# A hybrid backbone block on one core: the first channel tile's shift and scale columns are loaded apart, and the opening order of the tensor engine is rewritten

## The chip, the cores and the metric

The kernel runs on one core of one Trainium2 chip. The time is the device time of one execution in microseconds (us); the figure for the kernel before is the median of three runs. The engines are named as in the profile: PE is TensorE (matrix products), PEld its weight loads, DVE is VectorE, ACT is ScalarE, POOL is GpSimd, SP is SyncE, which here issues nearly all loads. SPq stands for its queue of load instructions.

## What is computed

One layer of a diffusion backbone over 512 latent tokens and 256 context tokens, model width 2048, all in 32-bit floats. Only the opening matters here:

```python
c_act = silu(c); cc_act = silu(c_ctx)
mod   = c_act  @ w_mod + b_mod          # 6 x 2048: sh1, sc1, gt1, sh2, sc2, gt2
mod_c = cc_act @ w_mod + b_mod
h  = rmsnorm(x,   g_norm1) * (1 + sc1)  + sh1
hc = rmsnorm(ctx, g_norm1) * (1 + csc1) + csh1
lat_in = h  @ w_in                      # q, k, v of 8 heads, gates
ctx_in = hc @ w_in
...
```

Behind it come two kinds of scans over the heads, an output projection, and a feed-forward part with a 3x3 convolution. They make up most of the time and are not touched.

## The kernel before

**Layout.** Channels lie on the 128 partitions: the 2048 channels are 16 channel tiles, numbered k, or 8 pairs, numbered kp. `xl[k]` is a tile of the 512 latent tokens (128 channels by 512 tokens), `xc[k]` one of the 256 context tokens. A product in full precision is made of three faster ones: each operand is split into a high part (a cast on ACT, `S.copy`, line 89) and a low part (a subtraction on DVE, line 90), and `mm3` adds high by high, high by low and low by high. In the profile `hTh` and `hTl` are the parts of the modulated latent tokens, `hch` and `hcl` those of the context, `hi_h` and `lo_h` those of a pair's weights of one head (`load_split`, line 160, 512 KB each).

**Order.** `pinned[0] = True` around `project_first` (lines 523 to 525) makes every product keep its program order on PE. So on PE what is written first runs first, and whatever stands behind a waiting product waits too. The other engines' order is set by the framework's scheduler, which prefers what stands under `tc.high_priority()`; `tc.issue_after(ins)` puts the instructions of a block behind `ins` on the engine of `ins`. Loads are issued by SP in program order; each needs a free buffer of its pool (`wraw` 4, `mraw` 7).

**The opening, in order.** (1) Three small loads (`cv`, a part of the constants, `cols`; lines 466 to 468) and then the 16 latent token tiles go out on SP (line 473). (2) `stream_rstd` (line 485): ACT squares each tile, DVE adds the squares up (`sq_l`, line 86), one product with a matrix of ones sums over channels (`ss_l`), and ACT and DVE turn the sum into `rl`, the reciprocal root for each token (`rstd` in the profile). (3) The shift and scale of a channel tile are needed as columns, one number for each partition. They come as rows first: `mod_rows` (line 221) multiplies the two condition vectors with 256 columns of `w_mod`, that is of one pair of channel tiles, in 32 instructions on PE (`ps_m`), and ACT copies the result to `rows_m`; `mod_cols` (line 234) transposes it with a small product for each tile, and DVE writes `scol` (scale, region 1) or `shcol` (shift, region 0). One `mod_load` (line 213) is four loads of 512 KB, for one region and one pair. (4) `modulate` (line 502) multiplies a tile by `rl`, applies scale and shift (line 510), and splits it. (5) Products: head 1 is accumulated pair by pair in banks that are evicted after each pair (`early_group`, `early_pair`; `psB`, two banks), head 0 in six banks that stay (`project_chunk`; `psA`, six banks). Groups 0 and 1 are q and k, groups 2 and 3 the latent v, groups 4 and 5 the context. `a` in the profile is any bank of a head.

In `project_first` (line 365) both regions of pair 0 are done first, then 8 products that nothing reads (line 379, they multiply ones with `rl`), then head 1's pair 0 groups 0 to 3, then head 0's, with the rows and columns of pair 1 and the context's sum (`ss_c`) set between them:

```python
        early_pair(w1, sums)
        for g in range(2, 4):
            early_group(0, g, w1, sums)
        project_chunk(0, *w0, banks[0], 0)
        rows = mod_rows(1, 1, raws[1])
        project_chunk(0, *w0, banks[1], 1)
        mod_cols(1, 1, *rows)
        ...
        rows = mod_rows(0, 1, raws[0])
        early_group(0, 4, w1, sums)
        mod_cols(0, 1, *rows)
        early_group(0, 5, w1, sums)
```

Then come the groups 4 and 5 of head 0 with the scale of pair 2, and a loop over pairs 1 to 7 with all six groups of head 1 and then of head 0 in each round. The shift and scale of the pairs ahead are set between the groups, some groups before they are needed.

Of the kernel before, what the change touches and what calls it, by code (L numbers as in the profile page):

```python
# [11 lines left out]
F32 = mybir.dt.float32  # L12
# [57 lines left out]
def block_kernel(ctx: ExitStack, tc: tile.TileContext, a: dict, out: bass.AP):  # L70
# [150 lines left out]
    def mod_rows(region, n, raws):  # L221

        bank = psb(f"ps_m{region}_{n}")
        ps = bank[:, 0:256]
# [4 lines left out]
        rows = tmp.tile([P, 256], F32, name=f"rows_m{region}_{n}", tag="rows")  # L229
# [4 lines left out]
    def mod_cols(region, n, bank, rows):  # L234
# [4 lines left out]
        with tc.high_priority():  # L239
            for b in range(2):  # L240
                k = 2 * n + b
                if region == 1:
                    V.tensor_scalar(out=scol[:, k, :], in0=pc[:, b, :], scalar1=bp1[:, k : k + 1],
                                    scalar2=gn1[:, k : k + 1], op0=ALU.add, op1=ALU.mult)
                else:
                    V.tensor_scalar(out=shcol[:, k, :], in0=pc[:, b, :], scalar1=bmod[:, k : k + 1],
                                    scalar2=None, op0=ALU.add)
# [61 lines left out]
    def project_chunk(kp, wh, wl, o, g, first=0, last=KT - 1):  # L309

        ks = list(enumerate((2 * kp, 2 * kp + 1)))
# [41 lines left out]
    def early_pair(w, sums):  # L353

        (wh, wl), ps = w, [psb(f"a1_0_{g}", BANKS[g]) for g in range(2)]
        for n, (ws, xs) in enumerate(((wh, hx[0]), (wl, hx[0]), (wh, hx[1]))):
            for k in range(2):
                for g in range(2):
                    mm(ps[g], ws[:, k, P * g : P * g + P], xs[k], start=(n == 0 and k == 0), stop=(n == 2 and k == 1))
        for g in range(2):  # L360
            sums[g] = actp.tile(list(BANKS[g]), F32, name=f"e0_{g}", tag=f"ah{KT - 4 + g}")
            with tc.high_priority():
                S.activation(sums[g], ps[g], AF.Copy, scale=SCALE if g == 0 else 1.0)

    def project_first():

        banks = [acc(f"a0_{g}", BANKS[g]) for g in range(6)]
        sums = [None] * 4 + [accp.tile([P, DK + DV], F32, name=f"e0_{4 + j}", tag=f"sum{j}") for j in range(CJ)]
        stream_rstd(xl, rl, "l", T)
        for r in (1, 0):  # L370
            mod_cols(r, 0, *mod_rows(r, 0, mod_load(r, 0)))
        w1, w0 = (load_split(a["w_heads"][h, 0], f"h{h}_0") for h in (1, 0))
        for j in range(KT // 2):
            nc.sync.dma_start(xcp[j], a["ctxT"][j])
        raws = {r: mod_load(r, 1) for r in (1, 0)}
        with tc.high_priority():
            ins = modulate(0, "x")

        for _ in range(8):
            mm(banks[5][:, 0:P], ones, rl[:, 0:P], start=True, stop=True)  # L380
        early_pair(w1, sums)
        for g in range(2, 4):
            early_group(0, g, w1, sums)
        project_chunk(0, *w0, banks[0], 0)
        rows = mod_rows(1, 1, raws[1])
        project_chunk(0, *w0, banks[1], 1)
        mod_cols(1, 1, *rows)
        with tc.high_priority(), tc.issue_after(ins):
            stream_rstd([x.rearrange("p a b -> p (a b)") for x in xcp], rc, "c", TC)
            ins = modulate(0, "c")  # L390
        for g in range(2, 4):
            project_chunk(0, *w0, banks[g], g)
        rows = mod_rows(0, 1, raws[0])
        early_group(0, 4, w1, sums)
        mod_cols(0, 1, *rows)
        early_group(0, 5, w1, sums)
# [3 lines left out]
        for r in (1, 0):  # L400
            raws[r] = mod_load(r, 2)
        nc.sync.dma_start(cst[:, 0:C_SA], a["consts"][:, 0:C_SA])
        project_chunk(0, *w0, banks[4], 4)
        rows = mod_rows(1, 2, raws[1])
        project_chunk(0, *w0, banks[5], 5)
        mod_cols(1, 2, *rows)
        for kp in range(1, KP):
            for g in range(6):
# [862 lines left out]
```

## Time and profile before

| | |
|---|---|
| three runs | 2586.46 to 2589.58 us, median 2588.95 |
| the profiled execution | 2584.39 us, its span from first to last instruction 2582.7 |
| mean granted clock of PE | 0.998 |
| DVE, ACT busy | 54%, 31% of the span |
| DMA over the span | 321.35 MB, mean 124 GB/s |
| chain of work that ended last | PE 91%, DVE 4%, DMA 2%, ACT 1%, issue 1% |

A row of the timeline has the start in us from the beginning of the span, the duration, the engine, the line, the operation, what it writes and reads, shapes and count; brackets hold the idle time of the engine before it and what released it. Matrix products are pipelined: the recorded duration of one is longer than the distance to the next. The line of every product is that of the helper `mm` (line 95), so products are told apart by their tiles. A product of 32-bit floats that aren't split takes two instructions.

### The profile page before, as it was taken

To read this page: it belongs to the slowest core of one execution; us is meant where nothing else is said; L and a number is where in the kernel's file an instruction comes from. 1 tells how busy PE (TensorE), PEld (TensorE's weight loads), DVE (VectorE), ACT (ScalarE), POOL (GpSimd) and SP (SyncE) were. 2 spreads that over 40 slices of the span, in tenths; PEclk is the share of its full clock that TensorE was granted. 3 is DMA by queue.
4 is the path that set the end of the run, shared out by engine and by line. 5 is a ranking of instruction groups with operands and counts; after the bars stand their busy time and mean duration, and the time that the engine had idled before them with its cause. 6 is when DMAs were issued, how large, how long until landed. Compare 5 with 4: busy or idle time off the path is not lost.

```text
span 2582.7 us, 31755 instructions
## 1 busy us (share of the span) xinstructions
PE 2533.8 (98%) x12944; PEld 2123.4 (82%) x12944; DVE 1400.4 (54%) x2055; ACT 811.3 (31%) x1209; POOL 78.5 (3%) x85
## 2 busy tenths in 40 slices
PE   6999999999999999999999999999999999999998
PEld 4887899888887888887788888888888888888887
DVE  6557765554445676459765336533653365336534
ACT  4224543322223242234533123312331233123332
POOL 0000000000000000002500000000000000000001
PEclk9999999999999999999999999999999999999999
DMA  9740011132335676324722222222232222222323
GB/s 383 273 156 34 33 42 50 42 122 98 114 115 186 245 266 239 131 85 147 272 97 97 98 98 98 95 96 95 98 98 98 98 98 93 95 97 87 105 94 106
DMA packets 96345, 321.35 MB, mean 124 GB/s; under 512 B 10884, under 2 KB 15304, under 8 KB 96200
## 3 DMA queue, kind: packets, MB, share of 16 engines
q1 hardware_dynamic: 95112, 318.29, 35.7%
q8 instruction: 101, 1.65, 0.3%
q10 hardware_dynamic: 1088, 1.05, 0.1%
q14 instruction: 44, 0.36, 0.0%
HBM read 315.10 MB, written 4.19 MB: 124 GB/s over the span
## 4 chain that ended last, share of the span: by engine, by line
PE 91%; DVE 4%; DMA 2%; ACT 1%; issue 1%; POOL 0%; SPq 0%; DVEq 0%; ACTq 0%; POOLq 0%
PE ug L95 17%; PE a L95 17%; PE dn L95 17%; PE uv L95 16%; PE ga L95 7%; PE wo L95 7%; PE po L95 3%; DMA raw_m<-in_w_mod 2%; PE ps_m L95 1%; PE sl L95 1%; PE dl L95 1%; DVE cv L1102 1%; DVE sum_m L268 0%; PE cst L95 0%; DVE sq_l L86 0%
## 5 line engine op out<-in xcount | busy, mean ns | idle before, releaser
L95 PE MATMUL uv<-h2h,lo_uv 128*128 128x512 f32 x688 | 268.1, 390 | 3.4 <-DVE lo_uv L90 3.4
L95 PE MATMUL ug<-h2h,lo_ug 128*128 128x512 f32 x688 | 266.7, 390 | 2.0 <-DVE lo_ug L90 2.0
L95 PE MATMUL uv<-h2h,hi_uv 128*128 128x512 f32 x688 | 267.8, 389 | 0.0
L95 PE MATMUL uv<-h2l,hi_uv 128*128 128x512 f32 x688 | 267.7, 389 | 0.0
L95 PE MATMUL ug<-h2h,hi_ug 128*128 128x512 f32 x688 | 267.5, 391 | 0.1
L95 PE MATMUL ug<-h2l,hi_ug 128*128 128x512 f32 x688 | 266.5, 389 | 0.0
L95 PE MATMUL dn<-gl,hi_d 128*128 128x512 f32 x644 | 250.6, 389 | 0.0
L95 PE MATMUL dn<-gh,hi_d 128*128 128x512 f32 x644 | 250.6, 389 | 0.0
L95 PE MATMUL dn<-gh,lo_d 128*128 128x512 f32 x644 | 250.6, 389 | 0.0
L1102 DVE SCALAR_TENSOR_TENSOR cv<-pad,cwt,cv 128x512 f32<-128x512 f32 x344 | 243.4, 762 | 9.0 <-ACT cv L1100 7.7
L90 DVE TENSOR_TENSOR lo_ug<-raw_ug,hi_ug 128x1024 fp32r<-128x1024 f32 (+1 forms) x88 | 106.9, 1214 | 254.9 <-ACT hi_ug L89 254.9
L90 DVE TENSOR_TENSOR lo_uv<-raw_uv,hi_uv 128x1024 fp32r<-128x1024 f32 (+1 forms) x88 | 109.8, 1247 | 176.3 <-ACT hi_uv L89 175.9
L268 DVE SCALAR_TENSOR_TENSOR sum_m<-raw_m,csil,sum_m 128x512 f32<-128x512 f32 x208 | 161.3, 775 | 55.6 <-DMA raw_m<-in_w_mod 51.4
L90 DVE TENSOR_TENSOR lo_d<-raw_d,hi_d 128x1024 fp32r<-128x1024 f32 x82 | 98.7, 1204 | 166.1 <-ACT hi_d L89 165.2
L89 ACT CAST hi_ug<-raw_ug 128x1024 fp32r<-128x1024 f32 (+1 forms) x88 | 90.8, 1032 | 276.3 <-PE ug L95 202.2
L89 ACT CAST hi_d<-raw_d 128x1024 fp32r<-128x1024 f32 x82 | 85.1, 1037 | 279.1 <-PE dn L95 224.4
L89 ACT CAST hi_uv<-raw_uv 128x1024 fp32r<-128x1024 f32 (+1 forms) x88 | 90.8, 1032 | 244.4 <-PE uv L95 182.0
L95 PEld LDWEIGHTS uv<-h2h,lo_uv 128*128 128x128 f32 x688 | 129.1, 188 | 31.6 <-DVE lo_uv L90 5.0
L95 PEld LDWEIGHTS ug<-h2h,lo_ug 128*128 128x128 f32 x688 | 129.1, 188 | 29.7 <-DVE lo_ug L90 2.8
L95 PEld LDWEIGHTS ug<-h2h,hi_ug 128*128 128x128 f32 x688 | 129.1, 188 | 27.9 <-issue 0.8
L95 PEld LDWEIGHTS uv<-h2l,hi_uv 128*128 128x128 f32 x688 | 129.1, 188 | 26.8
L95 PEld LDWEIGHTS uv<-h2h,hi_uv 128*128 128x128 f32 x688 | 129.1, 188 | 26.7
(312 smaller groups left out, 5018.6 us busy)
## 6 DMA issues: line engine op xcount, KB each, us to landing
raw_m<-in_w_mod SPq DMA_DIRECT2D x192, 512.0 KB, 4.6
raw_ug<-in_w_up SPq DMA_DIRECT2D x80, 512.0 KB, 3.2
raw_uv<-in_w_up SPq DMA_DIRECT2D x80, 512.0 KB, 3.3
raw_d<-in_w_down SPq DMA_DIRECT2D x79, 512.0 KB, 3.3
raw_h<-in_w_heads SPq DMA_DIRECT2D x64, 512.0 KB, 3.4
raw_ga<-in_w_gates SPq DMA_DIRECT2D x32, 512.0 KB, 3.5
raw_wo<-in_w_out SPq DMA_DIRECT2D x32, 512.0 KB, 3.2
xl<-in_xT SPq DMA_DIRECT2D x16, 256.0 KB, 5.4
```

The costliest lines, as they stand in the source:

```text
L89: S.copy(hi, x)
L90: return V.tensor_tensor(out=lo, in0=x, in1=hi.bitcast(F32), op=ALU.subtract).ins
L95: ins = PE.matmul(*args, **kw)
L268: V.scalar_tensor_tensor(out=dv, in0=x, scalar=ck, in1=dv, op0=ALU.mult, op1=ALU.add)
L1102: V.scalar_tensor_tensor(out=t3, in0=src, scalar=w, in1=t3, op0=ALU.mult, op1=ALU.add)
```

## The change

It does these things in `project_first` and its helpers, and in the three small loads:

- The three small loads are issued from ACT's queue (`nc.scalar.dma_start`) instead of SP's.
- Twelve products that nothing reads, on the first 256 tokens of latent tiles 2 to 13, are put ahead of `stream_rstd`.
- The rows of pair 0 are made tile by tile. A second arrangement of the same weights, `w_mod0`, holds them as two loads of 512 KB for each region and tile; `mod_half` makes rows of 128 columns and transposes them. Tile 0's loads stand ahead of the head weights, tile 1's behind them.
- `unread` products (three in each `mod_half` of tile 0, eight behind it) multiply ones with `rl`, as the eight of before did.
- With tile 0 alone come the products of head 0, groups 0 to 3, and of head 1, groups 0 and 1; then tile 1's rows, columns, modulation (`modulate_x`) and the same products again. Head 1's groups 0 and 1 take two `psA` banks for this.
- The context's sum and modulation are ordered behind tile 1's. Pair 1's scale is made and transposed between group 3 of head 1 and group 4 of head 0; its shift around the last group of head 1. Pair 2's scale moves into the loop's first round, and the load of pair 2's shift with it.

```diff
-    def mod_rows(region, n, raws):
+    def mod_load_half(region, k):
+
+        raws = []
+        for i in range(2):
+            pl = wraw if (region, k, i) == (0, 1, 1) else mraw
+            raws.append(pl.tile([P, 8, P], F32, name=f"raw_m{region}h{k}_{i}", tag="raw"))
+            nc.sync.dma_start(raws[-1], a["w_mod0"][k, region, i])
+        return raws
+
+    def mod_half(region, k, raws, o, n):
+
+        bank, rows = mod_rows(region, f"h{k}", [r[:, 4 * i : 4 * i + 4, :] for r in raws for i in range(2)], P)
+        unread(o, n)
+        pc = bank[:, 256:258]
+        mm(pc, rows, cc(C_SA, 2), start=True, stop=True)
+        with tc.high_priority():
+            mod_col(region, k, pc)
+
+    def unread(o, n, x=None):
+
+        x = rl[:, 0:P] if x is None else x
+        for _ in range(n):
+            mm(o[:, 0 : x.shape[1]], ones, x, start=True, stop=True)
+    def mod_rows(region, n, raws, w=256):
...
-        ps = bank[:, 0:256]
+        ps = bank[:, 0:w]
...
-        rows = tmp.tile([P, 256], F32, name=f"rows_m{region}_{n}", tag="rows")
+        rows = tmp.tile([P, w], F32, name=f"rows_m{region}_{n}", tag="rows")
...
+    def mod_col(region, k, pc):
+        if region == 1:
+            V.tensor_scalar(out=scol[:, k, :], in0=pc, scalar1=bp1[:, k : k + 1],
+                            scalar2=gn1[:, k : k + 1], op0=ALU.add, op1=ALU.mult)
+        else:
+            V.tensor_scalar(out=shcol[:, k, :], in0=pc, scalar1=bmod[:, k : k + 1],
+                            scalar2=None, op0=ALU.add)
...
-    def project_chunk(kp, wh, wl, o, g, first=0, last=KT - 1):
-
-        ks = list(enumerate((2 * kp, 2 * kp + 1)))
+    def project_chunk(kp, wh, wl, o, g, first=0, last=KT - 1, only=(0, 1)):
+
+        ks = [(kk, 2 * kp + kk) for kk in only]
...
-    def early_pair(w, sums):
-
-        (wh, wl), ps = w, [psb(f"a1_0_{g}", BANKS[g]) for g in range(2)]
-        for n, (ws, xs) in enumerate(((wh, hx[0]), (wl, hx[0]), (wh, hx[1]))):
-            for k in range(2):
+    def project_first():
+
+        pair = [acc(f"a1_0_{g}", BANKS[g]) for g in range(2)]
+        banks = [acc(f"a0_{g}", BANKS[g]) for g in range(4)]
+        sums = [None] * 4 + [accp.tile([P, DK + DV], F32, name=f"e0_{4 + j}", tag=f"sum{j}") for j in range(CJ)]
+        for k in range(2, 14):
+            unread(banks[3].rearrange("p a b -> p (a b)"), 1, xl[k][:, 0:256])
+        stream_rstd(xl, rl, "l", T)
+        halves = [[mod_load_half(r, 0) for r in (1, 0)]]
+        w0, w1 = (load_split(a["w_heads"][h, 0], f"h{h}_0") for h in (0, 1))
+        halves.append([mod_load_half(r, 1) for r in (1, 0)])
+        for j in range(KT // 2):
+            nc.sync.dma_start(xcp[j], a["ctxT"][j])
+        raws = {r: mod_load(r, 1) for r in (1, 0)}
+        for k in range(2):
+            for r, raw in zip((1, 0), halves[k]):
+                mod_half(r, k, raw, banks[3].rearrange("p a b -> p (a b)"), 3 if k == 0 else 0)
+            with tc.high_priority():
+                ins = modulate_x(k)
+            if k == 0:
+                unread(banks[3].rearrange("p a b -> p (a b)"), 8)
+
+            for n, (w, x) in enumerate(((0, 0), (1, 0), (0, 1))):
                 for g in range(2):
-                    mm(ps[g], ws[:, k, P * g : P * g + P], xs[k], start=(n == 0 and k == 0), stop=(n == 2 and k == 1))
+                    mm(banks[g], w0[w][:, k, P * g : P * g + P], hx[x][k], start=(k == 0 and n == 0), stop=False)
+            for g in range(2, 4):
+                project_chunk(0, *w0, banks[g], g, only=(k,))
+            for g in range(2):
+                project_chunk(0, *w1, pair[g], g, 0, 1, only=(k,))
         for g in range(2):
             sums[g] = actp.tile(list(BANKS[g]), F32, name=f"e0_{g}", tag=f"ah{KT - 4 + g}")
             with tc.high_priority():
-                S.activation(sums[g], ps[g], AF.Copy, scale=SCALE if g == 0 else 1.0)
-
-    def project_first():
-
-        banks = [acc(f"a0_{g}", BANKS[g]) for g in range(6)]
-        sums = [None] * 4 + [accp.tile([P, DK + DV], F32, name=f"e0_{4 + j}", tag=f"sum{j}") for j in range(CJ)]
-        stream_rstd(xl, rl, "l", T)
-        for r in (1, 0):
-            mod_cols(r, 0, *mod_rows(r, 0, mod_load(r, 0)))
-        w1, w0 = (load_split(a["w_heads"][h, 0], f"h{h}_0") for h in (1, 0))
-        for j in range(KT // 2):
-            nc.sync.dma_start(xcp[j], a["ctxT"][j])
-        raws = {r: mod_load(r, 1) for r in (1, 0)}
-        with tc.high_priority():
-            ins = modulate(0, "x")
-
-        for _ in range(8):
-            mm(banks[5][:, 0:P], ones, rl[:, 0:P], start=True, stop=True)
-        early_pair(w1, sums)
-        for g in range(2, 4):
-            early_group(0, g, w1, sums)
-        project_chunk(0, *w0, banks[0], 0)
-        rows = mod_rows(1, 1, raws[1])
-        project_chunk(0, *w0, banks[1], 1)
-        mod_cols(1, 1, *rows)
-        with tc.high_priority(), tc.issue_after(ins):
+                S.activation(sums[g], pair[g], AF.Copy, scale=SCALE if g == 0 else 1.0)
+        banks += [acc(f"a0_{g}", BANKS[g]) for g in range(4, 6)]
+        early_group(0, 2, w1, sums)
+        with tc.high_priority(), tc.issue_after(ins[0]), tc.issue_after(ins[1]):
             stream_rstd([x.rearrange("p a b -> p (a b)") for x in xcp], rc, "c", TC)
             ins = modulate(0, "c")
-        for g in range(2, 4):
-            project_chunk(0, *w0, banks[g], g)
+        early_group(0, 3, w1, sums)
+        mod_cols(1, 1, *mod_rows(1, 1, raws[1]))
+        project_chunk(0, *w0, banks[4], 4)
+        project_chunk(0, *w0, banks[5], 5)
+        early_group(0, 4, w1, sums)
         rows = mod_rows(0, 1, raws[0])
-        early_group(0, 4, w1, sums)
+        early_group(0, 5, w1, sums)
         mod_cols(0, 1, *rows)
-        early_group(0, 5, w1, sums)
         with tc.issue_after(ins):
             modulate(1, "xc")
         w1 = load_split(a["w_heads"][1, 1], f"h1_1")
-        for r in (1, 0):
-            raws[r] = mod_load(r, 2)
+        raws[1] = mod_load(1, 2)
         nc.sync.dma_start(cst[:, 0:C_SA], a["consts"][:, 0:C_SA])
-        project_chunk(0, *w0, banks[4], 4)
-        rows = mod_rows(1, 2, raws[1])
-        project_chunk(0, *w0, banks[5], 5)
-        mod_cols(1, 2, *rows)
         for kp in range(1, KP):
             for g in range(6):
+                if kp == 1 and g == 2:
+                    rows = mod_rows(1, 2, raws[1])
+                if kp == 1 and g == 3:
+                    mod_cols(1, 2, *rows)
                 if g == 5 and kp + 1 < KP:
                     rows = mod_rows(0, kp + 1, raws[0])
                 ins = early_group(kp, g, w1, sums)
                 if g == 2:
                     with tc.issue_after(ins):
                         w0 = load_split(a["w_heads"][0, kp], f"h0_{kp}")
+                    if kp == 1:
+                        raws[0] = mod_load(0, 2)
                     if kp + 2 < KP:
                         raws[1] = mod_load(1, kp + 2)
...
-    nc.sync.dma_start(cv, a["cvec"])
-    nc.sync.dma_start(cst[:, C_SA:], a["consts"][:, C_SA:])
-    nc.sync.dma_start(cols, a["cols"])
+    nc.scalar.dma_start(cv, a["cvec"])
+    nc.scalar.dma_start(cst[:, C_SA:], a["consts"][:, C_SA:])
+    nc.scalar.dma_start(cols, a["cols"])
...
+    def modulate_x(k):
+        mul(xl[k], xl[k], rl)
+        V.tensor_scalar(out=xl[k], in0=xl[k], scalar1=scol[:, k, 0:1], scalar2=shcol[:, k, 0:1], op0=ALU.mult, op1=ALU.add)
+        for part, t in zip(hx, "hl"):
+            part.append(acttile(k, t, f"hT{t}{k}"))
+        return S.copy(hx[0][k], xl[k]).ins, V.tensor_tensor(out=hx[1][k], in0=xl[k], in1=hx[0][k].bitcast(F32),
+                                                            op=ALU.subtract).ins
...
+    r["w_mod0"] = w_mod[0][:, : 2 * D].reshape(2, 8, P, 2, 8, 2, P)[:, :, :, :, 0].transpose(4, 3, 0, 2, 1, 5)
```

More of the change, by code (lines that the diff above doesn't have):

```diff
@@ L240, in mod_cols @@
             for b in range(2):
[L241 to L247, printed above, removed]
+                mod_col(region, 2 * n + b, pc[:, b, :])
+    def mod_col(region, k, pc):
[5 more added lines that the diff above has]
+                            scalar2=None, op0=ALU.add)
     def mod_chunk(region, n, kp, parts):
```

## The prediction

> **What bounds the kernel now.** I read the page first, then stretches of the span, then the timeline of the first 60 us.
>
> ```profile
> PE 2533.8 (98%) x12944; PEld 2123.4 (82%) x12944; DVE 1400.4 (54%) x2055; ACT 811.3 (31%) x1209; POOL 78.5 (3%) x85
> ```
>
> ```profile
> core 0 of [0], span 2582.7 us
> core 0: us, PE busy (x) PEld busy (x) DVE busy (x) ACT busy (x) POOL busy (x), PEclk, DMA share, GB/s
> 0.00:20.00 20.00, 0.38 (x1) 0.38 (x2) 12.73 (x24) 11.59 (x18) 0.20 (x4) 1.00 0.86 314
> 40.00:60.00 20.00, 19.76 (x168) 16.24 (x161) 12.99 (x32) 7.42 (x15) 0.00 (x0) 1.00 1.03 415
> ```
>
> PE is busy 98% of the span. It does next to nothing for 20 us (0.38), and soon after has almost no gap (19.76 of 20). So the end moves one for one with two things: when PE gets its first modulated channel tile, and every wait that opens behind that. The timeline shows the front, SP's queue first, then DVE and ACT, then PE (start, duration, what, in brackets the idle time before it and its releaser):
>
> ```profile
> 0.80 0.39 SPq L466 DMA_DIRECT2D cv<-in_cvec  x1
> ...
> 2.18 9.41 SPq L473 DMA_DIRECT2D xl<-in_xT  x16
> ```
>
> ```profile
> 5.74 0.63 ACT L490 ACTIVATE sq_l<-xl 128x512 f32<-128x512 f32 x1 [0.25 <-DMA xl<-in_xT]
> ...
> 10.11 9.45 DVE L86 TENSOR_TENSOR sq_l<-sq_l,sq_l 128x512 f32<-128x512 f32 x12 [0.43 <-ACT sq_l L490]
> ...
> 24.56 0.69 DVE L154 SCALAR_TENSOR_TENSOR rstd<-scr_l,rstd 128x512 f32<-128x512 f32 x1
> 24.78 0.37 ACT L231 COPY rows_m<-ps_m 128x256 f32<-128x256 f32 x1 [1.70 <-PE ps_m L95]
> ```
>
> ```profile
> 19.62 2.07 PE L95 MATMUL ss_l<-sq_l,cst 128*128 128x512 f32 x2 [19.62 <-DVE sq_l L86]
> 21.62 3.08 PE L95 MATMUL ps_m<-raw_m,cact 128*32 128x256 f32 x32
> 25.21 0.61 PE L95 MATMUL ps_m<-cst,rows_m 128*128 128x2 f32 x4 [0.50 <-ACT rows_m L231]
> 25.75 1.93 PE L95 MATMUL ps_m<-raw_m,cact 128*32 128x256 f32 x32
> 28.17 0.61 PE L95 MATMUL ps_m<-cst,rows_m 128*128 128x2 f32 x4 [0.49 <-ACT rows_m L231]
> 28.64 2.03 PE L95 MATMUL a<-rstd,cst 128*128 128x128 f32 x16
> 30.43 0.99 PE L95 MATMUL a<-hTh,hi_h 128*128 128x512 f32 x3
> ```
>
> DVE's last 12 adds of squares run back to back at 0.79 us and release the column sum ss_l at 19.62; rstd is done at 25.25. PE meanwhile does the scale rows (3.08), their transposition to columns, the shift rows (1.93), their transposition, and 8 unread products (16 instructions in 2.03 us, 0.13 each) that fill the wait for shift, scale and cast. The first real product starts at 30.43. The second batch of rows started at 25.75 with no load named as its releaser: what holds PE is this chain, not bytes.
>
> **The change part by part.** *Small inputs on ScalarE's queue.* The first token load is issued at 0.80 instead of 2.18: 1.38 us. ScalarE's three issues (0.39 for the first on SP) end near 2.1 and its table load behind them before the first square can run. Bounds: 0 (the landings stay, limited by the DMA engines) to 2.7 (15 adds of 0.79 behind the second square, which ended at 6.37 and would end near 5.0, so ss_l at 16.9). I take 1.4, the shift itself: ss_l at 18.2.
>
> *Twelve products on token tiles.* No such instruction is in the trace; they run while PE is idle and their price is nothing or a gain. The question is the clock. The profile page's DMA part gives a token load's time to landing, and one-microsecond stretches (busy time of PE, PEld, DVE, ACT, POOL, then the granted clock) show how it falls:
>
> ```profile
> xl<-in_xT SPq DMA_DIRECT2D x16, 256.0 KB, 5.4
> ```
>
> ```profile
> 210.00:211.00 1.00, 0.62 (x4) 0.52 (x4) 0.97 (x2) 0.74 (x2) 0.00 (x0) 1.00 0.00 0
> 211.00:212.00 1.00, 0.08 (x1) 0.00 (x0) 1.00 (x2) 0.82 (x3) 0.00 (x0) 0.87 0.00 0
> 212.00:213.00 1.00, 0.78 (x3) 0.78 (x4) 1.00 (x3) 0.40 (x1) 0.00 (x0) 0.50 0.00 0
> 218.00:219.00 1.00, 1.00 (x8) 1.00 (x8) 0.31 (x1) 1.00 (x2) 0.00 (x0) 0.72 0.00 0
> ```
>
> After two microseconds in which PE is busy 0.62 and 0.08, the granted clock falls to 0.50 and returns only in 218 to 219. In the front the column shows 1.00, but the first 32 row products took 3.08 us and the next 1.93, so they began slow. The last token tile with an unread product is the third from last: issued near 10.0 before, 1.4 earlier now, and landed 5.4 later, about 14 (an estimate). ss_l comes at 18.2. In those 4 nearly idle us the clock will most likely fall again. So I keep ss_l at 2.07: rstd at 25.25 - 1.4 = 23.9. If the clock held, 1.1 us less.
>
> *One tile of columns at a time.* For tile 0, PE's order is: scale rows of 128 columns, 3 unread products, transposition, shift rows, 3 unread, transposition, 8 unread, products. The unread products read rstd, so everything behind the first three waits for 23.9; the earlier landing of the halved weights buys nothing. From there: 6 instructions at half clock 1.5 (at full clock 6 x 0.13 = 0.8), transposition 0.3, half of 3.08 for the rows 1.5 (half of 1.93: 1.0), 3 unread at full clock 0.8 (they cover the 0.4 copy), and from the second transposition to the product 2.2, as from 28.17 to 30.43. Sum 6.3: first product at 30.2, against 30.43: **-0.2**. Bounds 26.5 (adds at 16.9, clock held) and 32.3 (half clock throughout).
>
> *Tile 1's columns now stand inside the product stream.* Before, both tiles' rows were done ahead of the first product. Now, after tile 0's 4.2 us of products, come two batches of rows (half of 1.93 each; at most 1.45 if the weight loads, which the halving leaves at 32, set the pace), two copies that nothing covers (0.35 each, somewhat under the 0.45 between 27.7 and 28.17), two transpositions 0.3, and 2.0 for shift and scale, cast and start. 2.0 + 0.7 + 0.3 + 2.0 = **+5.0** (4.5 to 5.9). This is real work or wait on PE, whose queue is in program order: everything stands behind it.
>
> *The context's sum is later.* Its squares are ordered behind tile 1's cast and its adds behind tile 1's split.
>
> ```profile
> 33.54 3.07 DVE L86 TENSOR_TENSOR sq_c<-sq_c,sq_c 128x512 f32<-128x512 f32 x4
> ```
>
> ```profile
> 33.93 0.39 PE L95 MATMUL a<-hi_h,hTh 128*128 128x256 f32 x1 [0.46 <-ACT e L363]
> ...
> 42.94 0.47 PE L95 MATMUL a<-hi_h,hTh 128*128 128x256 f32 x1
> ...
> 45.87 0.28 PE L95 MATMUL a<-hi_h,hTl 128*128 128x256 f32 x1
> ...
> 49.10 0.50 PE L95 MATMUL ps_m<-cst,rows_m 128*128 128x2 f32 x4
> 49.84 0.44 PE L95 MATMUL a<-hi_h,hch 128*128 128x384 f32 x1 [0.24 <-ACT e L349]
> ...
> 55.51 0.48 PE L95 MATMUL a<-hTh,hi_h 128*128 128x512 f32 x1
> ```
>
> Two squares (0.63 each) and seven adds (0.77 plus a gap, 0.79) end 6.8 us after tile 1's first product. PE reaches ss_c after 12 products of 512 columns and 24 of 256 (24 such run from 42.94 to 45.9, 0.12 each; twice that, 0.23, for 512): 5.6 us. **+1.2** (0 to 2).
>
> *Rows and columns of pair 1.* The scale rows are transposed at once, with nothing between: **+0.45**. The shift columns were transposed at 49.10 and used at 55.51, 6.4 us later. Now they are transposed right before the first product that needs them. Behind that transposition stand the shift and scale on DVE, the cast on ACT and the low part on DVE:
>
> ```profile
> 50.60 0.62 ACT L89 CAST hTh<-xl 128x512 fp32r<-128x512 f32 x1 [0.82 <-DVE xl L510]
> ...
> 51.26 0.69 DVE L90 TENSOR_TENSOR hTl<-xl,hTh 128x512 fp32r<-128x512 f32 x1
> ```
>
> The cast ended 2.1 us after the transposition began, the low part 2.85. The second product of the group reads the low part, the fourth and fifth read the next tile's, about 1 us later. The first group, 1.4 us of work, then ends some 4.6 us after the transposition began instead of 1.9: **+2.7** (2.2 to 3.5). The next pair's scale rows only change places.
>
> *What goes.* The 12 products of the old first pair took 3.50 us (30.43 to 33.93) for 2.77 of work, since the third group waited for the eviction of a bank; the 0.24 before 49.84 goes as well: **-1.0**. All other products are the same.
>
> *The clock at the new waits.* The wait ahead of pair 1 leaves PE idle for more than the 211 to 212 window showed, so I expect one fall there. That fall lasted 6.8 us and would cost about 3; half as long, with part of it in the wait, **+1.2** (0 to 5 with both waits).
>
> Here the Trainium skill speaks against one part of the sum and for another. "TensorE: Matmul & The Clock Gate", section "What's actually happening", says that the clock halves after at least one idle window of about 3.4 us. By that the 4 us gap can undo the unread token products, as I took it, while waits of 2 to 3 us would keep the clock and the sum would lack this last term. The trace disagrees with the second: its fall came with no such idle window.
>
> Sum: -0.2 + 5.0 + 1.2 + 0.45 + 2.7 - 1.0 + 1.2 = **+9.35 us**. The profiled execution took 2584.39 (its span 2582.7 and 1.7 around it), 4.6 under the median of 2588.95, so it becomes 2593.7 by its own measure; on the median, **2598.3**. Later stages start from PE's progress and shift with it.
>
> **Rivals.** (a) *No fall of the clock at the waits*: without 1.2, 2597.1. For it: the waits are broken by short products; against it: 210 to 213. This is also what the rule of the Trainium skill named above would give. (b) *Not slower by what can be told: the front moves by three us or more.* Place: adds and rstd. If the token tiles land close together and the clock holds until ss_l, rstd comes at 25.25 - 2.6 - 1.1 = 21.6 and the first product about 26.7, since the steps then run at full clock: -3.7 instead of -0.2, no fall later. 9.35 - 3.5 - 1.2 = +4.65, 2593.6. It decides from rstd before about 22. For it: 12 adds now wait only for each other; against it: the 4 idle us. (c) *Half clock throughout the front and at both waits*: +2 at the front, and 3 more at the waits: +14.5, 2603.5. For it: three broken stretches in 30 us; against it: the eight unread products. (d) Faster than before would need 8 us from the front; no row holds them.
>
> **How the numbers follow.** Forecast 0.45, (a) 0.15, (b) 0.20, (c) 0.16, (d) 0.04. About 0.2% (5.2 us) is what a measurement of this kernel can tell from no change. Below +5.2 lie (b) and a small part of (a): same 0.23; faster 0.04; slower 0.73. The range runs from +2.5, under (b) by its unknown landings, to +14.5, (c): 2591.5 to 2603.5.
>
> **What would show it.** Right: rstd done at 23 to 24.5; first product on tile 0 at 29.5 to 31; a gap of about 2 us on PE, released by the cast, ahead of tile 1's products; ss_c released by DVE; a wait of 2 us or more after the transposition ahead of pair 1; a granted clock of 0.50 near one of them. Wrong: a first product before 28, ss_l in about 1 us, or pair 1's products starting right behind the transposition.

## The result, and the profile after

The changed kernel takes 2599.86 us (median of 6 runs, 2596.06 to 2603.36), the kernel before 2588.69 beside it (6 runs, 2586.46 to 2590.02): 11.2 us more by the medians (a factor of 1.0043); the ratio on record, from all of these runs, is 1.005 (95% interval 1.0040 to 1.0061). The profiled execution took 2598.2 us, 13.8 more than that of before (2584.39). Its page, to be held against the page of before:

```profile
span 2596.5 us, 31954 instructions
...
PE 2552.2 (98%) x13044; PEld 2135.5 (82%) x13044; DVE 1401.6 (54%) x2055; ACT 811.3 (31%) x1211; POOL 78.0 (3%) x85
```

The shares are those of before. PE's busy time is 18.4 us longer, which is more than the loss, so busy time can't tell where the loss is (products at half clock are busy for longer, and the products on token tiles count too). A place that both kernels pass does. Head 0's gate products stand behind the whole first stage; this is their row in the tile view, first of before and then of the changed kernel (count, shortest/mean/longest ns, first to last start):

```profile
L95 PE MATMUL gm<-hch,wsm x32: 378/379/397, 196.6 to 199.5; 128*32 128x256 f32 x32
```

```profile
L95 PE MATMUL gm<-hch,wsm x32: 379/379/397, 211.6 to 214.5; 128*32 128x256 f32 x32
```

Already here 15.0 us are lost, and at the first product of pair 2 (76.07 before, 91.13 after) it was 15.1: all of the loss arises ahead of pair 2. Behind this row the changed kernel needs 1.2 us less. Now the front on PE's timeline, in the columns of the prediction's:

```profile
5.38 8.80 PE L95 MATMUL a<-xl,cst 128*128 128x256 f32 x24 [5.38 <-DMA xl<-in_xT]
17.72 2.08 PE L95 MATMUL ss_l<-sq_l,cst 128*128 128x512 f32 x2 [3.54 <-DVE sq_l L86]
19.72 1.94 PE L95 MATMUL ps_m_h<-raw_m1h,cact 128*32 128x128 f32 x32
23.41 1.65 PE L95 MATMUL a<-rstd,cst 128*128 128x128 f32 x6 [1.75 <-DVE rstd L154]
...
27.91 2.03 PE L95 MATMUL a<-rstd,cst 128*128 128x128 f32 x16
29.69 0.48 PE L95 MATMUL a<-hTh,hi_h 128*128 128x512 f32 x1
```

Read the brackets first. The column sum comes 1.9 us sooner (17.72 against 19.62) but takes 2.08, so the clock is still halved, after 3.54 idle us. The halved rows end near 21.7; then PE stands 1.75 us until rstd is there, for the unread products and for nothing else. Of 1.9 us gained, 0.74 reach the first product (29.69 against 30.43). Next, tile 1's columns:

```profile
34.15 1.08 PE L95 MATMUL ps_m_h<-raw_m1h,cact 128*32 128x128 f32 x32
35.67 0.38 PE L95 MATMUL ps_m_h<-cst,rows_m_h 128*128 128x2 f32 x2 [0.44 <-ACT rows_m_h L255]
35.98 1.08 PE L95 MATMUL ps_m_h<-raw_m0h,cact 128*32 128x128 f32 x32
37.51 0.38 PE L95 MATMUL ps_m_h<-cst,rows_m_h 128*128 128x2 f32 x2 [0.44 <-ACT rows_m_h L255]
39.43 0.50 PE L95 MATMUL a<-hTh,hi_h 128*128 128x512 f32 x1 [1.54 <-ACT hTh L536]
```

From 34.15 to 39.43 no product of the projection runs: 5.28 us. Then the context's sum and pair 1's scale rows, each with a wait, and the start of pair 1:

```profile
47.77 1.10 PE L95 MATMUL ss_c<-sq_c,cst 128*128 128x256 f32 x4 [0.92 <-DVE sq_c L86]
...
53.09 0.61 PE L95 MATMUL ps_m<-cst,rows_m 128*128 128x2 f32 x4 [0.93 <-ACT rows_m L255]
...
60.15 0.50 PE L95 MATMUL ps_m<-cst,rows_m 128*128 128x2 f32 x4
...
62.27 0.50 PE L95 MATMUL a<-hTh,hi_h 128*128 128x512 f32 x1 [1.61 <-ACT hTh L89]
63.67 0.50 PE L95 MATMUL a<-hTl,hi_h 128*128 128x512 f32 x1 [0.91 <-DVE hTl L90]
...
65.12 0.80 PE L95 MATMUL a<-hTh,hi_h 128*128 128x512 f32 x1 [0.71 <-ACT hTh L89]
...
74.68 0.38 PE L95 MATMUL a<-hi_h,hTh 128*128 128x256 f32 x1 [0.45 <-DVE e L377]
```

The shift columns are transposed at 60.15, and PE waits three times behind that: 1.61 for the cast, 0.91 for the low part, 0.71 for the next tile. At 74.68, behind pair 2's scale rows, it waits 0.45 more, for DVE to evict the bank of the group before. DVE's timeline of the same microseconds says why there are three:

```profile
61.02 0.54 DVE L547 TENSOR_SCALAR xl<-xl,scol,shcol 128x512 f32<-128x512 f32 x1
61.48 0.41 DVE L553 TENSOR_SCALAR xc<-xc,scol,shcol 128x256 f32<-128x256 f32 x1
61.80 1.22 DVE L90 TENSOR_TENSOR lo_h<-raw_h,hi_h 128x1024 fp32r<-128x1024 f32 x1
62.93 0.69 DVE L90 TENSOR_TENSOR hTl<-xl,hTh 128x512 fp32r<-128x512 f32 x1
...
63.87 0.54 DVE L547 TENSOR_SCALAR xl<-xl,scol,shcol 128x512 f32<-128x512 f32 x1
```

Between shift and scale (61.02) and the low part (62.93) stands a 1.22 us split of weights, and the next tile's shift and scale comes only at 63.87. Last, the granted clock (column behind POOL) in one-microsecond stretches of the changed kernel:

```profile
16.00:17.00 1.00, 0.00 (x0) 0.00 (x0) 0.79 (x3) 0.63 (x1) 0.00 (x0) 0.81 1.04 426
17.00:18.00 1.00, 0.28 (x1) 0.28 (x2) 0.66 (x1) 0.00 (x0) 0.00 (x0) 0.50 1.00 410
40.00:41.00 1.00, 1.00 (x5) 0.81 (x4) 0.64 (x2) 0.95 (x2) 0.00 (x0) 0.75 1.01 410
41.00:42.00 1.00, 1.00 (x6) 0.90 (x5) 0.48 (x2) 0.63 (x1) 0.00 (x0) 0.50 1.05 430
64.00:65.00 1.00, 0.41 (x2) 0.00 (x0) 0.74 (x2) 0.55 (x2) 0.00 (x0) 0.70 1.04 426
65.00:66.00 1.00, 0.88 (x2) 0.45 (x2) 0.90 (x2) 0.37 (x2) 0.00 (x0) 0.50 0.67 274
```

In the front it falls three times, in 16.6 to 26.9, 40.5 to 43.9 and 64.4 to 71.2, first in the 3.54 idle us ahead of the column sum, then 1.1 us behind the wait ahead of tile 1, then in the broken start of pair 1.

### The profile page after: what moved, and what is told of

It reads as the page before. It is cut to its first block, busy times and chain, and to the rows that moved or that the text cites. A ratio compares the mean times of both kernels' runs of the same rounds, so it can differ in the third digit from the quotient of the medians.

```text
span 2596.5 us, 31954 instructions
## 1 busy us (share of the span) xinstructions
PE 2552.2 (98%) x13044; PEld 2135.5 (82%) x13044; DVE 1401.6 (54%) x2055; ACT 811.3 (31%) x1211; POOL 78.0 (3%) x85
## 4 chain that ended last, share of the span: by engine, by line
PE 91%; DVE 5%; DMA 2%; issue 1%; ACT 1%; POOL 0%; DVEq 0%; ACTq 0%; POOLq 0%; SPq 0%
PE a L95 18%; PE ug L95 17%; PE dn L95 17%; PE uv L95 16%; PE wo L95 7%; PE ga L95 6%; PE po L95 4%; DMA raw_m<-in_w_mod 2%; PE sl L95 1%; PE dl L95 1%; PE ps_m L95 1%; DVE cv L1139 1%; DVE sum_m L294 1%; DVE sq_l L86 0%; PE cst L95 0%
## 5 line engine op out<-in xcount | busy, mean ns | idle before, releaser
L95 PE MATMUL a<-hi_h,hTh 128*128 128x256 f32 x512 | 151.0, 295 | 0.4 <-DVE e L377 0.4
```

Source lines behind the costliest of these rows:

```text
L95: ins = PE.matmul(*args, **kw)
```

## The experiments

The main theory: the loss is the sum of PE's waits for chains that this order puts right ahead of their use (tile 1's columns, the context's sum, pair 1's scale rows and shift columns), plus the clock's falls behind them, and the front gains little because the unread products wait for rstd. The rivals put the loss elsewhere: into the clock alone, into the loads, or into one unlucky execution. "At the gate row" below means the start of the row shown above (196.6 before, 211.6 changed). Ratios are to the kernel before, run beside each.

**Shift columns earlier (e1).** In the changed kernel pair 1's shift rows, their transposition and shift and scale move ahead:

```diff
         mod_cols(1, 1, *mod_rows(1, 1, raws[1]))
+        rows = mod_rows(0, 1, raws[0])
         project_chunk(0, *w0, banks[4], 4)
+        mod_cols(0, 1, *rows)
+        with tc.issue_after(ins):
+            modulate(1, "xc")
         project_chunk(0, *w0, banks[5], 5)
         early_group(0, 4, w1, sums)
-        rows = mod_rows(0, 1, raws[0])
         early_group(0, 5, w1, sums)
-        mod_cols(0, 1, *rows)
-        with tc.issue_after(ins):
-            modulate(1, "xc")
```

> The changed kernel with one thing moved: pair 1's shift rows are made right behind its scale columns and transposed behind group 4 of head 0, two groups and more ahead of the first product that needs them. Theory A (the loss is in waits that opened inside the product stream, the largest ahead of pair 1): the waits of 1.6, 0.9 and 0.7 us ahead of pair 1's products and the half clock from 64 to 71 us go; 5 to 7 us less than the changed kernel, about 2594. Rival B (the loss is in the front and in the split rows of tile 0 and 1, the wait ahead of pair 1 only shifts to the next place): at most 1 us less, about 2599.

PE's timeline at the start of pair 1, and the gate row:

```profile
59.91 0.40 PE L95 MATMUL a<-hTh,hi_h 128*128 128x512 f32 x1
...
61.60 0.50 PE L95 MATMUL a<-hTl,hi_h 128*128 128x512 f32 x1 [0.20 <-DVE hTl L90]
```

```profile
L95 PE MATMUL gm<-hch,wsm x32: 379/379/397, 204.9 to 207.8; 128*32 128x256 f32 x32
```

Of 3.23 us of waits 0.20 are left, the clock doesn't fall near 64, and the gate row comes 6.7 us sooner. At the context's sum only 0.3 of that was there (47.45 against 47.77), so some 6.4 us are the price of the place. The time is 2597.4 (5 runs, 2593.63 to 2598.76), 1.0032 [1.0019, 1.0044]: only 2.5 of the 6.7 show in the medians, less than was expected, and the intervals of the ratios overlap. How far the rest can be traced is told below the experiments.

**Tile 1's columns among tile 0's groups (e2).** In the changed kernel (`half_rows` and `half_cols` are `mod_half` taken in two; the loop around is shown in part):

```diff
...
+            if k == 0:
+                rows = half_rows(1, 1, halves[1][0])
             project_chunk(0, *w0, banks[2], 2, only=(k,))
+            if k == 0:
+                half_cols(1, 1, *rows)
+                rows = half_rows(0, 1, halves[1][1])
             project_chunk(0, *w0, banks[3], 3, only=(k,))
+            if k == 0:
+                half_cols(0, 1, *rows)
+                with tc.high_priority():
+                    ins = modulate_x(1)
...
```

> The changed kernel with tile 1's two batches of rows and their transpositions set between tile 0's groups, so that copies, shift, scale and cast run under products. Theory A: the waits of 0.44, 0.44 and 1.54 us ahead of tile 1 shrink to about 0.6 in all and the half clock that begins at 40.5 us goes; some is given back, since PE reaches the context's sum earlier against DVE's adds. 2 to 4 us less than the changed kernel, about 2597. Rival B (the rows themselves are the cost, their place is not): under 1 us less.

The waits ahead of tile 1 are gone, and the fall at 40.5 with them. From the first product on tile 0 (30.45 here, 0.8 later) to the context's sum (45.05) it takes 14.6 us instead of 18.1, although the wait for that sum grew from 0.92 to 1.35. The gate row starts at 207.8, 3.8 sooner; 2.7 of this were there at the context's sum. Pair 1's three waits stayed at 1.61, 0.91 and 0.71, but the clock's fall behind them lasted 3.4 us (62.6 to 66.0) instead of 6.8, which is the rest. Time 2598.14 (5 runs, 2593.35 to 2599.53), 1.0034 [1.0021, 1.0047], within the uncertainty of the changed kernel's.

**Only ScalarE's queue (e3).** In the kernel before, the three small loads alone:

```diff
-    nc.sync.dma_start(cv, a["cvec"])
-    nc.sync.dma_start(cst[:, C_SA:], a["consts"][:, C_SA:])
-    nc.sync.dma_start(cols, a["cols"])
+    nc.scalar.dma_start(cv, a["cvec"])
+    nc.scalar.dma_start(cst[:, C_SA:], a["consts"][:, C_SA:])
+    nc.scalar.dma_start(cols, a["cols"])
```

> The kernel before with one part of the change: the three small loads go out on ACT's queue. Theory A: ss_l starts about 1.9 us earlier, as in the changed kernel, and so does the first product; 1.5 to 2 us less than before, about 2587. Rival B (the front of before is held by the landing of the weights of the rows, or ACT's own issues delay it): within 0.5 us of before.

The column sum started at 17.70, as in the changed kernel (17.72), so the 1.9 us come from the queue alone (in the eleven profiles with this queue it starts anywhere from 17.65 to 18.98); the first product followed at 28.26. New waits for row weights appeared (0.20 and 0.62 near 37 to 39), and at the gate row 1.0 of the 2.2 us was left (195.6). Time 2586.09 (11 runs, 2581.78 to 2588.76), 0.9992 [0.9983, 1.0001]: a gain is likely and not proven.

**Holding the clock in the changed kernel (e4), and dropping the token products (e5).**

```diff
-        for k in range(2, 14):
-            unread(banks[3].rearrange("p a b -> p (a b)"), 1, xl[k][:, 0:256])
+        for k in range(2, 16):
+            unread(banks[3].rearrange("p a b -> p (a b)"), 1 if k < 15 else 5, xl[k][:, 0:256])
```

> The changed kernel with unread products on token tiles 14 and 15 too, five on the last, so that PE is busy nearly up to ss_l. Theory A (the clock fell at 16.6 us because PE was idle from 14.2 to 17.7): full clock from about 10 us to 35, ss_l in about 1.1 us instead of 2.1, first product 2 to 3 us earlier, 2 to 3 us less than the changed kernel, about 2597.4. Rival B (the clock of the front is a matter of the time from the start, not of idle time): no change in ss_l's 2.1 us and in the time.

PE's timeline of e4:

```profile
18.69 1.13 PE L95 MATMUL ss_l<-sq_l,cst 128*128 128x512 f32 x2 [1.45 <-DVE sq_l L86]
19.75 1.08 PE L95 MATMUL ps_m_h<-raw_m1h,cact 128*32 128x128 f32 x32
23.43 1.64 PE L95 MATMUL a<-rstd,cst 128*128 128x128 f32 x6 [2.61 <-DVE rstd L154]
...
29.72 0.48 PE L95 MATMUL a<-hTh,hi_h 128*128 128x512 f32 x1
```

The column sum takes 1.13 and the rows 1.08, so products up to the last token tile do hold the clock. But PE is then only sooner at the same wait, now 2.61 us, in which the clock falls (23.5 to 26.9), and the first product is no earlier: the expectation missed here. The token tiles landed about 1 us later in this execution, which hides a part. The time, 2598.48 (5 runs, 2595.57 to 2601.11), 1.0037 [1.0023, 1.0050], is the changed kernel's within the uncertainty. The gate row (208.9) is 2.7 us earlier for a reason that was not meant: DVE did the weight split ahead of the shift columns, so pair 1's second wait was 0.23 instead of 0.91, and the clock's fall there lasted 3.4 us instead of 6.8. In e2 it lasted 3.4 with DVE's order as it was, so its length does not follow from that order alone.

In e5 the loop over token tiles is left out.

> The changed kernel without its twelve unread products on token tiles. Theory A (they warm the clock only until the idle time from 14.2 to 17.7 us, and it falls before ss_l): ss_l again in 2.1 us, first product within 0.5 us of the changed kernel's, time the same within 1 us of the changed kernel in this call. Rival B (they are what lets the clock return at 27 us): first product 1.5 us later or more, time 1.5 to 3 us longer.

Without them the clock returned at 29.8 instead of 26.9, and from the column sum (17.85) to the first product (31.13) it took 13.3 us instead of 12.0. So the token products don't hold the clock, but with them it came back sooner: a gain that the prediction had at nothing. The first product, 1.4 us later, is near rival B's, the time is theory A's: 2598.25 (5 runs, 2594.77 to 2600.75), 1.0039 [1.0027, 1.0052]. DVE's order at pair 1 was again the other one, and no fall of the clock came there. PE's and then DVE's timeline:

```profile
64.85 0.50 PE L95 MATMUL a<-hTh,hi_h 128*128 128x512 f32 x1 [1.62 <-ACT hTh L89]
65.58 0.50 PE L95 MATMUL a<-hTl,hi_h 128*128 128x512 f32 x1 [0.23 <-DVE hTl L90]
```

```profile
64.38 0.54 DVE L545 TENSOR_SCALAR xl<-xl,scol,shcol 128x512 f32<-128x512 f32 x1
64.84 0.68 DVE L90 TENSOR_TENSOR hTl<-xl,hTh 128x512 fp32r<-128x512 f32 x1
```

The low part stands right behind shift and scale. A change 30 us earlier had reordered DVE's queue, and that alone moved about 1.7 us (worked out under *Pair 1* below); these two experiments therefore price the front only up to the first product.

**The changed kernel once more (e8).** Nothing is edited; a second profile tells what belongs to the order and what to one execution.

> The changed kernel once more, unaltered, beside the others: time near 2600, the waits of 0.4, 0.4 and 1.5 us ahead of tile 1 and of 1.6, 0.9 and 0.7 us ahead of pair 1 again (theory A); if they are another size or place, they were a matter of one execution (rival B).

The waits are the same: 0.44, 0.44 and 1.54 ahead of tile 1, 0.92 for the context's sum, 0.93 for the scale rows, 1.62, 0.91 and 0.71 at pair 1. So they belong to the order. The clock's falls do so only in part: at the same wait, tile 1's lasted 6.8 us (38.8 to 45.6) instead of 3.4. The first product starts at 30.28, 12.0 behind the column sum as in the first profile, the gate row at 213.3; the time is 2600.72 (5 runs, 2600.18 to 2602.30), 1.0051 [1.0038, 1.0063].

**All of the waits covered (e6).** e2 and e1 together, group 3 of head 1 ahead of the context's sum, and pair 1's shift rows between its scale rows and their transposition:

```diff
+        early_group(0, 3, w1, sums)
...
             ins = modulate(0, "c")
-        early_group(0, 3, w1, sums)
-        mod_cols(1, 1, *mod_rows(1, 1, raws[1]))
+        rows = mod_rows(1, 1, raws[1])
+        shift = mod_rows(0, 1, raws[0])
+        mod_cols(1, 1, *rows)
         project_chunk(0, *w0, banks[4], 4)
+        mod_cols(0, 1, *shift)
+        with tc.issue_after(ins):
+            modulate(1, "xc")
...
```

> The changed kernel with all four of its new waits covered: tile 1's rows between tile 0's groups, the context's sum behind group 3 of head 1, pair 1's shift rows between its scale rows and their transposition, its shift columns behind group 4 of head 0. Theory A: at the first product behind the opening it stands 11 to 13 us ahead of the changed kernel and about 2 to 4 us behind the kernel before; time 2590 to 2592. Rival B (the loss is bound to the split of pair 0's columns and stays): at least 6 us slower than before, 2594 or more.

```profile
L95 PE MATMUL gm<-hch,wsm x32: 378/379/397, 200.3 to 203.2; 128*32 128x256 f32 x32
```

11.3 of the 15.0 us at the gate row are back with the same work in another order. The time is 2592.37 (11 runs, 2589.41 to 2594.71), 1.0017 [1.0008, 1.0026], just above what theory A expected. With the same loads and the same products this leaves no room for bytes as the cause of the main part. The other 3.7 us stay; two batches of tile 1's rows still stand in the stream.

**Unread products that don't read rstd (e10), and with all waits covered (e9).** In the changed kernel, and then in e6 with e4's token products as well:

```diff
-        x = rl[:, 0:P] if x is None else x
+        x = xl[15][:, 0:P] if x is None else x
```

> The changed kernel with one thing altered: the three, three and eight unread products about tile 0's columns read a token tile instead of rstd. Theory A: the wait of 1.75 us ahead of the first three goes and the clock returns sooner; first product 2 to 4 us earlier, near 26.5, time 2 to 4 us less than the changed kernel, about 2597. Rival B: first product within 1 us of 29.7, because rstd, shift and cast on DVE and ACT are the chain in any case, or the loads are; no change in time.

PE's timeline of e10 has no wait for rstd left ahead of the first product:

```profile
18.20 1.80 PE L95 MATMUL ss_l<-sq_l,cst 128*128 128x512 f32 x2 [4.21 <-DVE sq_l L86]
...
26.56 0.73 PE L95 MATMUL a<-hTh,hi_h 128*128 128x512 f32 x2
```

One operand moves the first product from 29.69 to 26.56. At the gate row 1.6 of the 3.1 us are left (210.0): the fall at tile 1 lasted 6.8 us (35.6 to 42.4), as it did in e8 without any edit. The time is 2599.13 (5 runs, 2595.98 to 2602.94), 1.0047 [1.0034, 1.0059], is the changed kernel's within the uncertainty, and the expected 2 to 4 us didn't show.

> The kernel with all four waits covered, and besides: unread products on token tiles up to the last (five on it), and the unread products inside tile 0's columns read a token tile instead of rstd, so that they don't wait for it. Theory A (tile 0's split loads bought nothing because PE stood behind rstd, and the clock fell for it): first product on tile 0 near 25 us instead of 29.9, 4 to 5 us less than with the waits covered alone, about 2587.5, so at or under the kernel before. Rival B (the weights of tile 0 and of the heads land too late to use it, or later loads are then waited for): first product after 27.5, at most 2 us less, about 2590.5.

```profile
17.65 1.12 PE L95 MATMUL ss_l<-sq_l,cst 128*128 128x512 f32 x2 [0.72 <-DVE sq_l L86]
18.71 1.08 PE L95 MATMUL ps_m_h<-raw_m1h,cact 128*32 128x128 f32 x32
...
25.16 0.50 PE L95 MATMUL a<-hTh,hi_h 128*128 128x512 f32 x1 [0.51 <-ACT hTh L555]
```

Now the column sum takes 1.12, the halved rows 1.08, and the first product starts at 25.16, 5.3 us ahead of before; the clock is full from 10.2 to 211.6. The gate row starts at 195.8, 4.5 sooner than in e6. Both are near what theory A expected. Time 2587.48 (11 runs, 2585.43 to 2591.01), 1.0000 [0.9991, 1.0009]. So the idea of the change can be had without its loss, and then it ties with the kernel before: in e9 the early front of 5.3 us shrinks to 0.8 at the gate row.

**The old order with the queue and a held clock (e7).** The kernel before with e3's edit, and behind each token tile from the third on one unread product, five on the last:

```diff
+        for k in range(2, 16):
+            for _ in range(1 if k < 15 else 5):
+                mm(banks[3].rearrange("p a b -> p (a b)")[:, 0:256], ones, xl[k][:, 0:256], start=True, stop=True)
```

> The kernel before with the small loads on ACT's queue and unread products on token tiles 2 to 15 (five on the last), nothing else. There PE doesn't wait for rstd between ss_l and the second batch of rows. Theory A: clock held, ss_l in 1.1 us instead of 2.1 and the first rows in 1.9 instead of 2.7, first product near 26.5 us (28.3 with the queue alone, 30.4 before); 3 to 4 us less than before, about 2584.5. Rival B (the weights of the rows then land too late): PE waits for a load ahead of the second batch, first product near 27.5, 2 us less than before as with the queue alone.

```profile
18.48 1.12 PE L95 MATMUL ss_l<-sq_l,cst 128*128 128x512 f32 x2 [0.92 <-DVE sq_l L86]
19.54 1.93 PE L95 MATMUL ps_m<-raw_m,cact 128*32 128x256 f32 x32
...
24.05 0.64 PE L95 MATMUL ps_m<-raw_m,cact 128*32 128x256 f32 x8 [0.48 <-DMA raw_m<-in_w_mod]
25.26 0.64 PE L95 MATMUL ps_m<-raw_m,cact 128*32 128x256 f32 x8 [0.58 <-DMA raw_m<-in_w_mod]
```

The first batch of rows takes 1.93 instead of 3.08, and the second then runs into its loads (0.48 and 0.58): a wait that a halved load might shorten exists, but only once PE is this early (that was not tried). The first product starts at 28.65, not near 26.5: this step went as rival B had it. Time 2584.37 (11 runs, 2581.15 to 2588.11), 0.9989 [0.9980, 0.9998]: the best version here, 3.9 us under the kernel before by the medians of those runs (2588.29), with an interval that nearly touches 1. That the time is theory A's is luck, since the front isn't: e3 had its first product at 28.26. At the gate row e7 is at 195.4 and e3 at 195.6, so a gain from holding the clock, over the queue alone, isn't shown.

**Where gains went behind the gate row.** From that row to the end of the span the twelve profiled executions (before, changed, e1 to e10) need 2384.9 to 2393.5 us, though the same work is done there. Sorted by the half clock in that part:

| half clock behind the gate row | us to the end |
|---|---|
| 3.4 us (e5) | 2386.7 |
| 6.8 (before, changed, e7) | 2386.1, 2384.9, 2385.1 |
| 10.2 (e3, e4, e8) | 2390.0, 2390.5, 2385.7 |
| 13.7 (e1, e2, e10) | 2392.1, 2388.6, 2387.6 |
| 17.1 (e6, e9) | 2390.2, 2393.5 |

More half clock goes loosely with more time. The same product in e6 and in before:

```profile
797.35 1.23 PE L95 MATMUL po<-c,qs 128*128 128x258 f32 x2 [3.21 <-DVE ed L83]
```

```profile
793.62 0.70 PE L95 MATMUL po<-c,qs 128*128 128x258 f32 x2 [2.10 <-DVE ed L83]
```

In before the wait is 2.10 us and the clock stays; in e6 it is 3.21 and the clock is halved from 796.1 to 802.9. A fall near 800 or 1155 comes in all of the other eleven executions and not in that of before. Half clock costs at most half its length, so the 6.9 us more of it in e1 account for at most 3.4 of the 7.2 us by which e1 is slower here than the changed kernel; the rest stays open. Whether an earlier front provokes the falls or they come by chance isn't settled by one profile for each kernel; e8, the unaltered changed kernel, had two of its three at other places than its first profile.

## Why the prediction was right

The sign, the place and the order of the loss were as forecast; 2598.3 was forecast, 2599.86 measured. By its steps, measured by the profiled executions up to the first product of pair 2, where 15.06 us are lost against 9.35 forecast:

| step | forecast | measured |
|---|---|---|
| first product on tile 0 | -0.2 | -0.74 |
| tile 1's columns in the stream | +5.0 | +5.28 (34.15 to 39.43) |
| clock behind them | 0 | +1.6 (39.43 to 46.68, 7.25 in place of 5.6) |
| the context's sum | +1.2 | +0.92 |
| pair 1's scale rows | +0.45 | +0.93 |
| pair 1's shift columns, with the clock | +2.7 + 1.2 | +7.0 (12.07 in place of 5.08) |
| pair 2's scale rows | 0 | +0.6 (wait at 74.68) |
| what goes | -1.0 | -1.0 |
| sum | +9.35 | +14.6; 0.5 not assigned |

*Front.* Rstd was done at 23.35 (23.9 forecast), PE waited 1.75 us for it with unread products next in its queue, and the halved weights bought nothing. e10 shows that this reading of the queue was the right one: with another operand the same kernel gains 3.1 us here. Token products were put at nothing: e5 gives them 1.3. Rival (b) needed rstd before 22 and a full clock at the column sum; neither came, and in e4 a full clock there was not enough, since rstd gates the rest (in that execution the column sum began 1 us later).

*Tile 1.* The term was right to 0.3 us; its wait ahead of the first product is 1.54, released by the cast, where a gap of about 2 us was forecast. e2 takes it out. The fall of the clock behind it was put at nothing and cost 1.6.

*Pair 1: the term that was mis-sized*, 3.9 forecast and 7.0 measured. No single wait reached the 2 us that were forecast (1.61), but there were three. The sum took DVE's low part right behind the cast, as before; DVE did a 1.22 us split of weights between, which delayed the low part and the next tile. And the clock's fall here lasted 6.8 us where half of that was taken. No run moved the split alone, but the runs with the same products here tell the parts apart. The time is that from the transposition of pair 1's shift to the first product behind pair 2's scale rows; in before, where these rows stand elsewhere, the two pieces are added (55.15 to 58.36 and 52.12 to 53.99).

| run | DVE's split | half clock here | time | more than before |
|---|---|---|---|---|
| before | behind the low part | none | 5.08 | |
| e5 | ahead of the shift | none | 7.69 | 2.6 |
| e4 | ahead of the shift | 3.4 us | 9.23 | 4.1 |
| e2 | ahead of the low part | 3.4 us | 10.89 | 5.8 |
| changed | ahead of the low part | 6.8 us | 12.07 | 7.0 |

So the chain itself cost 2.6 and its 2.7 was right. The split, of which the sum knew nothing, cost about 1.7, and the clock about 2.7 (1.5 for the first 3.4 us, 1.2 for the second) instead of 1.2. e1 takes nearly all of it away together.

*Pair 2's scale rows* "only change places" in the prediction. They now hold one of the two `psB` banks between two groups of head 1, and the next group waits 0.45 us for the eviction of the other; all eight experiments on the changed kernel have this wait too (0.44 or 0.45).

*Clock.* At the new waits one fall was expected, ahead of pair 1; there were two, tile 1's being the other, so rival (a) fell. The Trainium skill, "TensorE: Matmul & The Clock Gate", section "What's actually happening", has the clock halve after an idle window of about 3.4 us. Here it fell twice where no single gap was longer than 1.61 us, so the trace disagrees with a full idle window as the condition; but every fall that ends inside these traces lasts 3.4, 6.8 or 10.2 us, which agrees with 3.4 as the unit. The waits alone don't decide it: behind 1.61 and 0.23 us at pair 1 the clock fell in e4, behind 1.62 and 0.23 it didn't in e5. Where no gap was longer than 0.92 us, in e7 and e9 from 11.4 to 211, it didn't fall.

*The total.* Terms of 14.6 and a total of 11.2 don't contradict each other: behind the gate row the changed kernel's execution was 1.2 us quicker, and the execution of before that served as base lies under all of its timed runs (2584.39; 2586.46 to 2590.02). The forecast is 5.7 us under at pair 2 and 4.5 under the profiled execution (2593.7 against 2598.2). That it lies 1.6 from the median is in good part luck.

## What to carry to other kernels

When an engine with an in-order queue is busy 98% of the time, price each chain that a new order places right ahead of its use at its full latency, and read what else the helper engine has queued between the links: the chain's own instructions were priced right here, a split queued between them and the clock behind the waits were missed. Instructions that are only there to fill a wait must not read a value from the chain whose wait they fill. Split a first load only where the trace shows the engine waiting for the bytes; here the other queue alone brings the old order 1.0 us at the gate row (e3), and the split order, with all of its waits covered and its unread products freed of rstd, is 0.8 ahead there and ties in time (e9).

## What was not expected of the hardware

- Waits of 1.5 us, broken by short products, can halve the clock, and the fall then costs as much again as the wait (1.6 us at tile 1). They don't always: e4 and e5 differ with the same waits.
- Issuing a load from ScalarE takes about as long as from SyncE (0.39 in before's first row of SP's queue, 0.40 to 0.47 here); ScalarE's queue in the changed kernel:

```profile
0.80 0.40 ACTq L495 DMA_DIRECT2D cv<-in_cvec  x1
1.23 0.47 ACTq L496 DMA_DIRECT2D cst<-in_consts  x1
1.74 0.46 ACTq L497 DMA_DIRECT2D cols<-in_cols  x1
```

- The same code behind the gate row takes 2384.9 to 2393.5 us, a scatter of 8.6 us, with 3.4 to 17 us of half clock at changing places that explain a part of it. Below some 3 us a gain in the front of this kernel is best read at a row that both versions pass, and the medians of 11 runs say whether it reaches the end.
